# Every second low-part subtraction on GpSimd, and one layer's scale and shift summed on VectorE

## The chip, the cores and the metric

The kernel runs on one core of one Trainium2 chip, as one launch. The metric is the device time of that core in microseconds (us); less is better. The kernel before took 2017.45 us (median of 3 runs, 2016.82 to 2020.26).

## What is computed

The reference is a trunk of two layers over 256 tokens with 2048 features, all in float32. Each layer has a mixer and a feed-forward; each of the four takes `modulate(rmsnorm(x))` and adds its gated output to `x`. Shift, scale and gate come from the conditioning vector `c`: six vectors of 2048 per layer, each `silu(c)` times a 2048x2048 piece of `ada_w`, plus a bias.

```python
cond = jax.nn.silu(c)
for l in range(DEPTH):
    mod = cond @ ada_w[l] + ada_b[l]
    sh1, sc1, g1, sh2, sc2, g2 = jnp.split(mod, N_MOD, axis=-1)
    h = modulate(rmsnorm(x, norm_mix_g[l]), sh1, sc1)
    y = mixer_ab(...) if l % 2 == 0 else mixer_c(...)
    x = x + g1[:, None, :] * y
    h = modulate(rmsnorm(x, norm_ffn_g[l]), sh2, sc2)
    x = x + g2[:, None, :] * swiglu(h, ffn_w1[l], ffn_w3[l], ffn_w2[l])
return rmsnorm(x, final_g)
```

Mixer AB (layer 0) has a projection to 4096 columns, a causal convolution of width 31 over 1024 channels with LayerNorm and SiLU, a gated product with a causal 128x128 mixing of tokens, and a projection back. Mixer C (layer 1) is a causal pooling with one small product per group of channels. The feed-forward is a SwiGLU with 5632 hidden features.

## The kernel before

Tokens stand in two blocks of 128. Every dense product keeps the transposed activations stationary and streams a weight as the moving operand. A product in float32 is made of three in float32r: a weight is cut into `hi = round(w)` and `lo = w - hi`, the activations likewise, and hi*hi, lo*hi and hi*lo are added up in PSUM.

The grain of the work is a unit (`unit`, or `block` for several in one go): SyncE loads 512x512 of a weight (1 MB, `load`, L180) into one of five `raw` buffers; in two halves of 128x1024 `split` (L160) casts `hi` on ScalarE (L165) and subtracts `lo` on VectorE (L166); TensorE then runs, per half, eight matmuls with `hi` (L203, L204) and four with `lo` (L209). There are four `hi` and four `lo` buffers, so the cuts run up to four halves ahead of the products. Up to the end of mixer C the kernel has 184 units: 32 of the projection in, 16 of the projection back, 132 of the first feed-forward and 4 of the pooling mixer. The last feed-forward has another 132.

Two kinds of work run beside the units. `filler` (called five times per half, L167) issues the convolution, which is 31 VectorE instructions for each of 8 channel tiles (L655, L660), and then its LayerNorm. `tick` (L267) issues background steps, 1.2 per unit in mixer AB and 0.71 in the first feed-forward: each step loads 1 MB of `ada_w` for a modulation vector. On TensorE (`on_pe`, L305 and L379) a step is 16 small float32 matmuls, each recorded as two instructions. On VectorE (`weighed`, L349 and L351) it is two passes over 128x1024, `acc = raw * cond + acc`, and TensorE only adds up over the partitions at the end (`put_cols`, L408).

In mixer AB the background order is: the gate g1 on TensorE (L305), then the columns of scale and shift of the first feed-forward on TensorE (`norm_cols` with `mod_cols`, L379), in eight parts of 512 columns. In the first feed-forward it is the gate g2 and the modulation of layer 1, on VectorE. GpSimd has the norms' powers (L472, L748, L690), memsets, and the four bands for mixer C (`bands`, L123 to L149), which are built there during the first feed-forward.

The order of the instructions on each engine comes from a scheduler that takes them by priority as the operands come free; `soon` raises the priority of a phase's entry.

Of the kernel before, what the change touches and what calls it, by code (L numbers as in the profile page):

```python
# [8 lines left out]
F32 = mybir.dt.float32  # L9
# [5 lines left out]
P = 128  # L15
# [23 lines left out]
class Trunk:  # L39
    """Activations stand in [token, feature] blocks of 128 tokens; every dense product keeps  # L40
    the transposed activations stationary and streams a weight as the moving operand.

    A float32 operand w is cut into two float32r parts, hi = round(w) and lo = w - hi, and a
    product is hi*hi + hi*lo + lo*hi, added up in float32 in PSUM."""

    def __init__(self, ctx, tc, ins, out):
        self.ctx, self.tc, self.nc = ctx, tc, tc.nc
        self.i, self.out = ins, out
        self.bg = []
        self.credit = 0.0  # L50
        self.late = []
        self.fill = []

        def pool(name, bufs, **kw):
            return ctx.enter_context(tc.tile_pool(name=name, bufs=bufs, **kw))

        self.cpool = pool("const", 1)
        self.xpool = pool("resid", 1)
        self.apool = pool("act", 1)
        self.rawp = pool("raw", RAW)  # L60
        self.hip = pool("whi", HL)
        self.lop = pool("wlo", HL)
        self.accp = pool("acc", 1)
        self.gp = pool("gate", 2)
        self.wk = pool("work", 2)
        self.mmp = pool("mmp", 4, space=PSUM)
        self.tpp = pool("tpp", 2, space=PSUM)
        self.adap = pool("adap", 1, space=PSUM)
        self.msp = pool("msp", 1, space=PSUM)

# [52 lines left out]
    def bands(self, tiles):  # L123
        """band[w][:, 0 and 1] takes the first 128 tokens to the trailing mean over w tokens
        minus the token, for both halves of the sequence; band[w][:, 2] the second 128 to the
        second half; band[w][:, 3] has the sums over the columns of the first, which from column
        w - 1 on are those of every later token."""
        nc = self.nc
        self.band = {}
        for w, t in zip(WINDOWS, tiles):  # L130
# [3 lines left out]
            # token s (partition) counts for token n (free) when n - w < s <= n  # L134
# [16 lines left out]
    def load_rows(self, src):  # L151
        """A vector as rows of 512 at partitions 0, 32, 64, 96, zeros elsewhere."""
        t = self.wk.tile([P, 512], F32, name="brow", tag="brow", bufs=1)
        self.nc.gpsimd.memset(t, 0.0)
        n = src.shape[0] // 512
        self.nc.sync.dma_start(out=t[0 : 32 * n : 32, :], in_=src.rearrange("(j n) -> j n", n=512))
        return t

# [1 line left out]
    def split(self, raw, h):  # L160
# [5 lines left out]
        nc.vector.tensor_tensor(lo, part, hi.bitcast(F32), op=ALU.subtract)  # L166
# [4 lines left out]
    def filler(self):  # L171
        """One instruction of the work that runs between the cuts of the weights."""
# [15 lines left out]
    def unit(self, w, row0, col0, act, ps, first, last):  # L188
        """ps[b] += act[b] @ w[row0 : row0 + 512, col0 : col0 + 512]; act[b] = (hi, lo)."""
# [23 lines left out]
    def block(self, cells, hooks={}):  # L213
        """Units in one go, the first 128 tokens through all of them before the others.
        hooks[b, n]: what is issued ahead of half unit n of tokens b."""
# [23 lines left out]
    def tail(self, cells, resid, entry):  # L239
        """The last units of a phase: the next one's entry begins with the first 128 tokens  # L240
        while the others are still on."""
# [10 lines left out]
    def soon(self, f, *args):  # L252
        """f(*args), ahead of what else the engines could take up by then."""
        with self.tc.high_priority(SOON):
            f(*args)
# [36 lines left out]
    def mod(self, l, v, on_pe, then):  # L292
        """One modulation vector, silu(c) @ ada_w + ada_b; then(rows) gets it as four rows
        of 512, at partitions 0, 32, 64, 96."""
# [39 lines left out]
    def weighed(self, acc, l, col0):  # L334
        """acc[p, n] = the sum over k of cond[k * 128 + p] * ada_w[k * 128 + p, col0 + n]"""
# [21 lines left out]
    def mod_full(self, l, v, dst, gname=None, halves=(0, 1)):  # L357
        """A modulation vector, or half of it, as columns; see mod_cols."""
# [7 lines left out]
    def mod_cols(self, l, v, q, on_pe, dst, gname=None):  # L366
        """Part q (512 entries) of a modulation vector as columns, dst[p, k] = mod[k * 128 + p],
        or gain * (1 + mod) with a gain."""
# [54 lines left out]
    def to_bcast(self, rows, dst, n=4):  # L423
        """dst[p, :] = vector, on every partition"""
# [11 lines left out]
    def norm_cols(self, e, l, sc, sh, gname, sc_pe, sh_pe):  # L436
        """The columns of gain * (1 + scale) and of shift, in four parts each."""
# [6 lines left out]

    def bcast(self, l, v, on_pe, dst, times=None):
        """A modulation vector (times another) on every partition."""
# [9 lines left out]
    def sumsq(self, b, q):  # L456
        """The squares of a part of the residual, added up as soon as it stands."""
# [17 lines left out]
    def transposed(self, b, q, r):  # L475
        """A PSUM bank with part q of x[b] * r, transposed."""
# [17 lines left out]
    def scaled(self, src, q, b, gs, sh):  # L494
        """gs * src + sh, split: k-tiles 4q to 4q + 3 of the stationary operand."""
# [13 lines left out]
    def prep_norm(self, e, b, q):  # L509
        """act[q][b]: rmsnorm(x) * gain * (1 + scale) + shift, transposed and split."""  # L510
        e.act[q][b] = self.scaled(self.transposed(b, q, e.r[b]), q, b, e.gs, e.sh)

    def prep_late(self, e, b, q):
        """prep_norm, but for the last part, whose scale and shift come later."""
        (self.prep_norm if q < 3 else self.prep_plain)(e, b, q)

    def prep_plain(self, e, b, q):
        """The transposed x * rstd, to wait for scale and shift."""
# [4 lines left out]
    def started(self, e, w_cols, rate, then=None):  # L523
        """The first products of a layer by parts of 512 features, each as soon as its part of
        scale and shift has come."""
# [18 lines left out]
    def begun(self, e, w_cols, rest):  # L544
        """The first products of a layer, over three parts of the features and then over the
        last, as soon as its scale and shift have come."""
# [22 lines left out]
    def to_act(self, src, hi, lo):  # L569
        """src [128 tokens, 512] to split k-tiles."""  # L570
# [17 lines left out]
    def mixer_ab(self, e, nxt):  # L588
        nc, i = self.nc, self.i
        with ExitStack() as s:  # L590
# [19 lines left out]
            def params():  # L610
                """The small parameters of the mixer, laid out."""
# [54 lines left out]
            def norm_a():  # L666
                """LayerNorm over the channels, which stand on the partitions, and SiLU."""
# [45 lines left out]
            # A: gated halves, transposed to [channel, token]  # L713
# [21 lines left out]
            # B: values, normed over channels, mixed over the tokens of a chunk  # L735
# [69 lines left out]
    def prep_pool(self, e, b, g):  # L805
        """The pooling runs along the tokens, so it is a product with a band over them that leaves
        the features on the partitions, where scale and shift then go in: with n = rmsnorm(x),
        band' (gs * n + sh) = gs * (band' n) + sh * (the sums over the band's columns)."""
# [8 lines left out]
        t = self.wk.tile([P, 512], F32, name="xc", tag="xc", bufs=3)  # L817
# [120 lines left out]
    def finish_out(self, b, r):  # L938
        """The last norm; its gain is in already, but for the last part."""
# [12 lines left out]
    def run(self):  # L952
# [24 lines left out]
        self.norm_cols(ffn0, 0, SC2, SH2, "ffn_g", True, True)  # L977
# [4 lines left out]
        with ExitStack() as s:  # L982
# [15 lines left out]
            self.rate = RATES[4]  # L998
            self.g2 = self.gate()
# [6 lines left out]
class Entry:  # L1006
    """What a phase needs before its first product: the norm's factor per 128 tokens, then
    parts of 512 features, prepared one by one."""
# [50 lines left out]
```

## Time and profile before

| | |
|---|---|
| median of 3 runs (lowest, highest) | 2017.45 us (2016.82, 2020.26) |
| profiled execution: span | 2018.1 us |
| TensorE busy | 1961.8 us, 97% |
| VectorE busy | 1384.8 us, 69% |
| ScalarE busy | 837.0 us, 41% |
| GpSimd busy | 36.2 us, 2% |
| mean granted TensorE clock | 0.984 |

The page gives no other time for the profiled execution than its span, which stands 0.65 us above the median. PE is TensorE's matmuls, PEld its weight loads, DVE is VectorE, ACT ScalarE, POOL GpSimd, SP SyncE. Matmuls are pipelined and their ends are modelled, so PE can read as busy while it does not run at its full rate; the number of matmuls in a stretch says more. By lines and times, the program falls into these stages: the start to about 161 us; the convolution beside the first 24 or so units of mixer AB, 161 to 336; the rest of mixer AB, 336 to 443; the first feed-forward, 443 to 1205; mixer C, to about 1260; the last feed-forward, to the end.

### The profile page before, as it was taken

What the parts mean: (1) busy time and instruction counts of PE and PEld (TensorE: products, weight loads), DVE (VectorE), ACT (ScalarE), POOL (GpSimd) and SP (SyncE); (2) the same over time, 40 slices, a digit from 0 to 9 for tenths busy, and PEclk for the clock granted to TensorE, in tenths of its full rate; (3) what the DMA queues carried; (4) which work ended last, traced back from release to release, by engine and by line L of the source; (5) the groups of instructions that cost most, each with busy time, mean ns of one, the idle gap of its engine ahead of it and who ended that gap; (6) DMA issues with size and microseconds to landing.
All of it is one profiled execution on the core that took longest, in us unless ns stands there. A gap on an engine that the chain in (4) does not pass through costs nothing.

```text
span 2018.1 us, 23297 instructions
## 1 busy us (share of the span) xinstructions
PE 1961.8 (97%) x9039; PEld 1542.1 (76%) x9039; DVE 1384.8 (69%) x1660; ACT 837.0 (41%) x1025; POOL 36.2 (2%) x91
## 2 busy tenths in 40 slices
PE   4889999999999999999999999999999999999998
PEld 2457677668887888887878887788788888888886
DVE  3668998556777788777877788777455444554455
ACT  2333333445444343433343346544433444334443
POOL 1000000000000000000120000000000000000000
PEclk7889999999999999999999999999999999999999
DMA  9997887877888898888888886888555555555552
GB/s 327 329 380 278 318 297 285 304 283 254 286 305 316 319 330 321 306 308 313 307 322 303 301 299 232 307 319 312 187 188 187 188 188 188 187 188 190 190 188 78
DMA packets 240159, 540.30 MB, mean 268 GB/s; under 512 B 8393, under 2 KB 9721, under 8 KB 237616
## 3 DMA queue, kind: packets, MB, share of 16 engines
q1 hardware_dynamic: 238264, 536.94, 75.1%
q10 hardware_dynamic: 1784, 1.86, 0.3%
q8 instruction: 71, 1.16, 0.2%
q14 instruction: 40, 0.33, 0.0%
HBM read 536.68 MB, written 2.10 MB: 267 GB/s over the span
## 4 chain that ended last, share of the span: by engine, by line
PE 94%; DVE 2%; DMA 2%; ACT 1%; issue 0%; POOL 0%; POOLq 0%; SPq 0%; ACTq 0%; DVEq 0%
PE mm L203 28%; PE mm L204 28%; PE mm L209 27%; PE ps_ada L379 3%; PE ps_col L408 2%; PE tp L574 1%; DVE accq L388 1%; DMA x<-in_x_dram 1%; PE ps_ada L305 1%; PE mt L204 1%; PE mt L203 1%; PE mt L209 1%; PE tp L823 1%; DVE lo L166 1%; PE tp L482 0%
## 5 line engine op out<-in xcount | busy, mean ns | idle before, releaser
L166 DVE TENSOR_TENSOR lo<-raw,hi 128x1024 fp32r<-128x1024 f32 x632 | 768.4, 1223 | 435.6 <-ACT hi L165 430.7
L165 ACT CAST hi<-raw 128x1024 fp32r<-128x1024 f32 x632 | 661.1, 1053 | 930.9 <-PE mm L204 808.5
L203 PE MATMUL mm<-hi,ah 128*128 128x512 f32 x1600 | 632.3, 395 | 8.6 <-ACT hi L165 7.4
L204 PE MATMUL mm<-hi,al 128*128 128x512 f32 x1600 | 625.9, 391 | 0.0
L209 PE MATMUL mm<-lo,ah 128*128 128x512 f32 x1600 | 431.9, 390 | 2.2 <-DVE lo L166 2.2
L203 PEld LDWEIGHTS mm<-hi,ah 128*128 128x128 f32 x1600 | 301.7, 189 | 96.4 <-ACT hi L165 15.2
L209 PEld LDWEIGHTS mm<-lo,ah 128*128 128x128 f32 x1600 | 301.0, 188 | 66.2 <-DVE lo L166 3.3
L204 PEld LDWEIGHTS mm<-hi,al 128*128 128x128 f32 x1600 | 302.1, 189 | 61.9 <-issue 0.8
L203 PE MATMUL mm<-hi,hh 128*128 128x512 f32 x704 | 279.3, 397 | 0.0
L204 PE MATMUL mm<-hi,hl 128*128 128x512 f32 x704 | 277.9, 395 | 0.0
L351 DVE SCALAR_TENSOR_TENSOR acc<-raw,cond,acc 128x1024 f32<-128x1024 f32 x180 | 230.4, 1280 | 8.7 <-DMA raw<-in_ada_w_dram 7.2
L209 PE MATMUL mm<-lo,hh 128*128 128x512 f32 x704 | 194.6, 395 | 0.0
L203 PEld LDWEIGHTS mm<-hi,hh 128*128 128x128 f32 x704 | 132.1, 188 | 33.4 <-issue 0.8
L209 PEld LDWEIGHTS mm<-lo,hh 128*128 128x128 f32 x704 | 132.1, 188 | 32.2
L204 PEld LDWEIGHTS mm<-hi,hl 128*128 128x128 f32 x704 | 132.1, 188 | 31.2
L660 DVE SCALAR_TENSOR_TENSOR co<-aT,cw,co 128x256 f32<-128x256 f32 x240 | 99.1, 476 | 0.0
L582 DVE TENSOR_TENSOR gy<-mm,gate 128x512 f32<-128x512 f32 x72 | 46.9, 685 | 49.6 <-PE mm L209 49.6
L379 PE MATMUL ps_ada<-raw,cond 128*32 128x512 f32 x448 | 71.8, 677 | 5.6 <-DMA raw<-in_ada_w_dram 5.6
L203 PE MATMUL mm<-hi,mh 128*128 128x512 f32 x160 | 65.9, 413 | 0.0
L204 PE MATMUL mm<-hi,ml 128*128 128x512 f32 x160 | 63.1, 395 | 0.0
L388 DVE SCALAR_TENSOR_TENSOR accq<-raw,cond,accq 128x512 f32<-128x512 f32 x84 | 57.6, 744 | 0.0
L583 DVE TENSOR_TENSOR x<-x,gy 128x512 f32<-128x512 f32 x72 | 47.1, 686 | 0.2
(164 smaller groups left out, 939.9 us busy)
## 6 DMA issues: line engine op xcount, KB each, us to landing
raw<-in_ffn_w_dram SPq DMA_DIRECT2D x264, 1024.0 KB, 5.0
raw<-in_ada_w_dram SPq DMA_DIRECT2D x192, 1024.0 KB, 6.7
raw<-in_ab_w_in_dram SPq DMA_DIRECT2D x32, 1024.0 KB, 6.9
raw<-in_ab_w_out_dram SPq DMA_DIRECT2D x16, 1024.0 KB, 6.1
raw<-in_pool_w_dram SPq DMA_DIRECT2D x4, 1024.0 KB, 5.4
x<-in_x_dram SPq DMA_DIRECT2D x2, 1024.0 KB, 17.6
gate<-in_final_g_dram SPq DMA_DIRECT2D x1, 1024.0 KB
out_dram<-x SPq DMA_DIRECT2D x2, 512.0 KB, 3.7
```

The costliest lines, as they stand in the source:

```text
L165: nc.scalar.copy(hi, part)
L166: nc.vector.tensor_tensor(lo, part, hi.bitcast(F32), op=ALU.subtract)
L203: nc.tensor.matmul(ps[b], act[b][0][:, kk, :], hi[:, k, :], start=first and kk == 0, stop=False)
L204: nc.tensor.matmul(ps[b], act[b][1][:, kk, :], hi[:, k, :], start=False, stop=False)
L209: self.nc.tensor.matmul(ps[b], act[b][0][:, kk, :], lo[:, k, :], start=False, stop=last and kk == 3)
L351: nc.vector.scalar_tensor_tensor(acc, r2[:, j, :], self.cond[:, k : k + 1], acc, op0=ALU.mult, op1=ALU.add)
L379: nc.tensor.matmul(acc[32 * j : 32 * j + 32, :], self.cond[:, k : k + 1].to_broadcast([P, 32]), raw[:, j, :], start=u == 0, stop=u == 3, s ...
L388: nc.vector.scalar_tensor_tensor(acc[:, k % 2, :], raw[:, j, :], self.cond[:, k : k + 1], acc[:, k % 2, :], op0=ALU.mult, op1=ALU.add,)
L408: nc.tensor.matmul(ps[:, a : a + 1], src[:, P * a : P * a + P], one, start=u == 0, stop=u == len(parts) - 1,)
L582: nc.vector.tensor_tensor(t, ps, g[:, 512 * q : 512 * q + 512], op=ALU.mult)
L583: nc.vector.tensor_tensor(xs, xs, t, op=ALU.add)
L660: nc.vector.scalar_tensor_tensor(co[:, k, :], src, cw[:, k, j : j + 1], co[:, k, :], op0=ALU.mult, op1=ALU.add,)
```

## The change

Of the two halves of each unit, the second has its `lo` subtracted on GpSimd instead of VectorE, until the flag `shared` is cleared, which happens after mixer C. The columns of scale and shift of the first feed-forward are no longer summed by TensorE in parts of 512 but by VectorE in halves of 1024 (`norm_halves` with `mod_full`, which the kernel already has for layer 1). The accumulator `acc` gets a second buffer; the tile `xc` of mixer C takes turns in the buffers of `s1` and `hm` instead of three of its own. Comments are left out, which moves line numbers: `lo` is L168 in the changed kernel, the accumulation L351 and L353, the convolution L668 and L673.

```diff
+        self.shared = True
...
-        self.accp = pool("acc", 1)
+        self.accp = pool("acc", 2)
...
         nc.scalar.copy(hi, part)
-        nc.vector.tensor_tensor(lo, part, hi.bitcast(F32), op=ALU.subtract)
+        eng = nc.gpsimd if h and self.shared else nc.vector
+        eng.tensor_tensor(lo, part, hi.bitcast(F32), op=ALU.subtract)
...
+    def norm_halves(self, e, l, sc, sh, gname):
+
+        e.parts = []
+        for hh in range(2):
+            e.parts += [
+                self.add(
+                    self.mod_full(l, sc, e.gs, gname, (hh,)), self.mod_full(l, sh, e.sh, None, (hh,))
+                ),
+                (),
+            ]
...
-        t = self.wk.tile([P, 512], F32, name="xc", tag="xc", bufs=3)
+        t = self.wk.tile([P, 512], F32, name="xc", tag=("s1", "hm")[b])
...
-        self.norm_cols(ffn0, 0, SC2, SH2, "ffn_g", True, True)
+        self.norm_halves(ffn0, 0, SC2, SH2, "ffn_g")
...
             self.mixer_c(mix1, ffn1)
             self.rate = RATES[4]
+            self.shared = False
```

On VectorE, late in the convolution of mixer AB, this is a piece of the order before (`co` is the convolution's output, `lo` the low part of a weight half, `sh` the shift's columns):

```order
L660 SCALAR_TENSOR_TENSOR co<-aT,cw,co 128x256
L166 TENSOR_TENSOR lo<-raw,hi 128x1024
L414 TENSOR_TENSOR sh_140<-ps_col,adab 128x4
L660 SCALAR_TENSOR_TENSOR co<-aT,cw,co 128x256 x7
L166 TENSOR_TENSOR lo<-raw,hi 128x1024
L660 SCALAR_TENSOR_TENSOR co<-aT,cw,co 128x256 x3
L166 TENSOR_TENSOR lo<-raw,hi 128x1024
L660 SCALAR_TENSOR_TENSOR co<-aT,cw,co 128x256 x7
```

The same place on VectorE after the change, just behind the first `bo` pair (`acc` is the new accumulation of the feed-forward's scale and shift):

```order
L673 SCALAR_TENSOR_TENSOR co<-aT,cw,co 128x256 x9
L351 TENSOR_SCALAR acc<-raw,cond 128x1024
L673 SCALAR_TENSOR_TENSOR co<-aT,cw,co 128x256
L353 SCALAR_TENSOR_TENSOR acc<-raw,cond,acc 128x1024
L673 SCALAR_TENSOR_TENSOR co<-aT,cw,co 128x256
L353 SCALAR_TENSOR_TENSOR acc<-raw,cond,acc 128x1024
L168 TENSOR_TENSOR lo<-raw,hi 128x1024
L353 SCALAR_TENSOR_TENSOR acc<-raw,cond,acc 128x1024
L673 SCALAR_TENSOR_TENSOR co<-aT,cw,co 128x256 x8
L353 SCALAR_TENSOR_TENSOR acc<-raw,cond,acc 128x1024
L168 TENSOR_TENSOR lo<-raw,hi 128x1024
```

A subtraction stands there once per unit instead of twice, and about two accumulations per unit have come in. All 64 passes of the accumulation (4 of L351, 60 of L353) stand ahead of the first feed-forward's first subtraction on VectorE.

On GpSimd, from the norm of the start to the entry of the first feed-forward, the order before is this (`r`, `m` and `rv` are the norms' factors, `brow` a buffer for a bias):

```order
L472 TENSOR_TENSOR r<-m,mhalf 128x1 x2
L154 MEMSET brow 128x512
L748 TENSOR_TENSOR m<-m,mhalf 128x1 x2
L690 TENSOR_TENSOR rv<-rv,mhalf 128x2
L472 TENSOR_TENSOR r<-m,mhalf 128x1 x2
```

And after the change, over the same stretch:

```order
L485 TENSOR_TENSOR r<-m,mhalf 128x1 x2
L168 TENSOR_TENSOR lo<-raw,hi 128x1024 x22
L155 MEMSET brow 128x512
L168 TENSOR_TENSOR lo<-raw,hi 128x1024 x3
L761 TENSOR_TENSOR m<-m,mhalf 128x1 x2
L168 TENSOR_TENSOR lo<-raw,hi 128x1024 x10
L703 TENSOR_TENSOR rv<-rv,mhalf 128x2
L168 TENSOR_TENSOR lo<-raw,hi 128x1024 x13
L485 TENSOR_TENSOR r<-m,mhalf 128x1 x2
```

The powers of the norms now stand in one queue with the subtractions, 48 of which lie ahead of the first feed-forward's norm. Over the whole program GpSimd gets 184 of them, one per unit; the bands for mixer C come behind the 145th, in two batches with a single subtraction between them.

## The prediction

> **What bounds the kernel now.** I read the engines' totals first, then the busy time by stage, then the waits, then the single rows where GpSimd and VectorE run at the same time. The totals, from the page:
>
> ```profile
> span 2018.1 us, 23297 instructions
> PE 1961.8 (97%) x9039; PEld 1542.1 (76%) x9039; DVE 1384.8 (69%) x1660; ACT 837.0 (41%) x1025; POOL 36.2 (2%) x91
> ```
>
> TensorE is the bound on average. The windows by stage (convolution; rest of mixer AB; first twelve units of the feed-forward; the rest of it; mixer C; last feed-forward) say where another engine is close. The columns are the stretch and its length, then PE, PEld, DVE, ACT and POOL busy with counts:
>
> ```profile
> 161.00:336.00 175.00, 175.00 (x888) 121.06 (x887) 166.50 (x324) 61.80 (x84) 2.93 (x3) 1.00 0.84 302
> 336.00:443.00 107.00, 107.00 (x543) 76.68 (x542) 60.16 (x76) 42.83 (x62) 1.61 (x1) 0.98 0.84 302
> 443.00:510.00 67.00, 65.24 (x317) 51.82 (x316) 46.22 (x65) 40.64 (x59) 2.00 (x2) 1.00 0.67 233
> 510.00:1205.00 695.00, 695.00 (x3133) 568.09 (x3132) 548.86 (x535) 284.93 (x307) 21.02 (x61) 1.00 0.87 310
> ```
>
> In the convolution stretch VectorE is busy 166.50 of 175 us, 95%: there both engines are full. In the rest of mixer AB it is 60.16 of 107, in the feed-forward 595.08 of 762 (78%). The waits of the whole run, with total, times and longest:
>
> ```profile
> ACT hi L165 <- PE mm L204: 808.5, 491, 6.4
> DVE lo L166 <- ACT hi L165: 430.7, 356, 3.3
> PE mm L203 <- ACT hi L165: 7.4, 3, 4.2
> ```
>
> The cuts wait for TensorE to free their buffers, and TensorE waits only 7.4 us for a cut. So outside the convolution a lighter VectorE gains nothing by itself; what can gain is less work on TensorE.
>
> **What TensorE loses.** L379 in mixer AB is the matmuls of the feed-forward's scale and shift:
>
> ```profile
> 161.00:336.00 175.00, 14.49 (x112) 2.40 (x112) 1.00 0.84 302
> 336.00:443.00 107.00, 15.55 (x120) 2.55 (x120) 0.98 0.84 302
> ```
>
> That is 14.49 + 15.55 = 30.0 us off the path between 161 and 443 us (a few more lie just behind). The column sums stay: 8 parts of 4 small matmuls become 4 of 8. If nothing took its place, the 282 us of mixer AB would become 252, and the run 1988.
>
> **What VectorE gains and loses.** The costs of one instruction (busy us in all, mean ns of one; the last two rows serve further down), and how many cuts lie in each stretch (windows of L166), are
>
> ```profile
> L166 DVE TENSOR_TENSOR lo<-raw,hi 128x1024 fp32r<-128x1024 f32 x632 | 768.4, 1223 | 435.6 <-ACT hi L165 430.7 <-PE mm L209 3.2
> L351 DVE SCALAR_TENSOR_TENSOR acc<-raw,cond,acc 128x1024 f32<-128x1024 f32 x180 | 230.4, 1280 | 8.7 <-DMA raw<-in_ada_w_dram 7.2
> L349 DVE TENSOR_SCALAR acc<-raw,cond 128x1024 f32<-128x1024 f32 x12 | 9.0, 746 | 0.0
> L660 DVE SCALAR_TENSOR_TENSOR co<-aT,cw,co 128x256 f32<-128x256 f32 x240 | 99.1, 476 | 0.0
> L906 DVE TENSOR_TENSOR hm<-s,mm 128x512 f32<-128x512 f32 x44 | 28.3, 682 | 11.9 <-PE mm L209 11.9
> L576 DVE TENSOR_TENSOR hl<-tp,hh 128x512 fp32r<-128x512 f32 x44 | 28.2, 681 | 2.6 <-ACT hh L575 2.6
> ```
>
> ```profile
> 161.00:336.00 175.00, 55.61 (x46) 1.00 0.84 302
> 336.00:443.00 107.00, 33.17 (x28) 0.98 0.84 302
> 443.00:510.00 67.00, 28.10 (x23) 1.00 0.67 233
> 510.00:1205.00 695.00, 293.94 (x241) 1.00 0.87 310
> ```
>
> Mixer AB from 161 us on: half of 74 cuts, 37, leave VectorE: half of 88.78, 44.4 us. In come 60 x 1.280 + 4 x 0.746 = 79.8 us. VectorE's 226.7 us become 262.1. First feed-forward: half of 264 cuts leave, half of 322.0, 161 us; 595.1 become 434.
>
> **What GpSimd costs VectorE.** No row of before shows a 128x1024 subtraction on GpSimd, so its price is bounded, and the first question is whether it runs beside VectorE at all. While the bands are built, VectorE has these rows:
>
> ```profile
> 1003.11 1.28 DVE L582 TENSOR_TENSOR gy<-mm,gate 128x512 f32<-128x512 f32 x2
> 1004.31 1.55 DVE L583 TENSOR_TENSOR x<-x,gy 128x512 f32<-128x512 f32 x2
> 1005.78 1.48 DVE L166 TENSOR_TENSOR lo<-raw,hi 128x1024 fp32r<-128x1024 f32 x1
> ...
> 1008.32 1.30 DVE L351 SCALAR_TENSOR_TENSOR acc<-raw,cond,acc 128x1024 f32<-128x1024 f32 x1
> 1009.55 1.30 DVE L166 TENSOR_TENSOR lo<-raw,hi 128x1024 fp32r<-128x1024 f32 x1
> ```
>
> and GpSimd these:
>
> ```profile
> 1003.81 0.54 POOL L141 TENSOR_SCALAR_AFFINE_SELECT bandhl<-bandhl 128x128 f32<-128x128 f32 x2
> 1004.33 1.85 POOL L145 TENSOR_TENSOR bandhl<-bandhl,ident 128x128 f32<-128x128 f32 x2
> ...
> 1007.25 3.76 POOL L136 TENSOR_SCALAR_AFFINE_SELECT bandhh<-bandhh 128x128 f32<-128x128 f32 x3
> ...
> 1019.23 0.87 POOL L145 TENSOR_TENSOR bandhl<-bandhl,ident 128x128 f32<-128x128 f32 x2
> ```
>
> Beside `gy`, which reads PSUM and one SBUF tile, two selects take 0.54 us. Beside `lo` and `acc`, which read two SBUF tiles, three take 3.76, each about as long as the VectorE instruction it meets. It works both ways: the two `x` additions take 1.55 where the equal pair `gy` takes 1.28, and the `lo` behind them 1.48 where its group's mean is 1.22. Each is 0.26 to 0.27 late, and one subtraction of the bands goes in ahead of each. So I take the two engines as one resource for instructions that read two SBUF tiles: one runs, the other stands. Convolution, cuts, accumulations and the residual's addition are all of that kind.
>
> The price of one new subtraction in this resource: the 128-column one held VectorE for 0.26 to 0.27 us, so 1024 columns hold it for 8 times that, about 2.15 us. The ends come from these rows (min, median and max in ns; and one select over 1024 columns, 1091 ns):
>
> ```profile
> L145 POOL TENSOR_TENSOR bandhl<-bandhl,ident x4: 447/684/978, 1004.3 to 1019.7; 128x128 f32<-128x128 f32 x4
> L612 POOL TENSOR_SCALAR_AFFINE_SELECT prm<-prm 128x1024 f32<-128x1024 f32 x1 | 1.1, 1091 | 11.8 <-DMA prm<-in_b_w_s_dram 11.8
> ```
>
> With one input, 1024 columns took 1.09 us, so about 1.0 is the low end for two; the undisturbed 0.447, times 8, is 3.6, the high end. I take 2.15, since it is the same operation's own hold. The Trainium skill prices it apart from these rows: GPSIMD Engine Reference, section 3.1 (Elementwise), has 4497 ns for an add of 2048 float32 columns, by which I estimate 2.25 us for 1024; no run here shows it, and by it the sum below would be 4 us longer in mixer AB.
>
> **Mixer AB, the sum.** 37 x 2.15 = 79.6 us of GpSimd on top of VectorE's 262.1 is 341.7 us, for a stretch that lasted 282 and in which TensorE now needs 252. What can lie side by side are VectorE's PSUM reads, above all `gy`, with 15 instructions there (windows of L582, the feed-forward's rows for below):
>
> ```profile
> 336.00:443.00 107.00, 9.70 (x15) 0.98 0.84 302
> 443.00:510.00 67.00, 0.69 (x1) 1.00 0.67 233
> 510.00:1205.00 695.00, 14.13 (x22) 1.00 0.87 310
> ```
>
> So 332 to 342; I take 337, which is **55 us longer**. The pair now sets the pace, and the 30 us saved on TensorE vanish under it. What waits then: behind a held VectorE instruction stand `gy` and the next cut, for which TensorE waits; behind a held GpSimd cut the next cut and the norms' powers; and a `raw` buffer stays taken until its last cut is through, so SyncE's next load starts later. Ends: 262.1 + 37 x 1.0 less 9.7 is 289, 7 longer; with 3.6 it is 395, over 100 longer.
>
> **First feed-forward, the sum.** 434 + 132 x 2.15 = 284 makes 718 us, and of GpSimd's 21.0 us there before I count 12 as bands that read SBUF, an estimate: 730 of 762, 96%. Up to 43 of it are PSUM reads that can lie beside GpSimd: 14.8 of `gy`, and of `hm` and `hl` the first feed-forward's half, 14.2 and 14.1. So the pair still fits, but with 4 to 10% to spare, where VectorE had 22%, and with four buffers to even things out. I take **12 us** of stalls, between 0 and 30. One more place is priced apart: the bands stand in GpSimd's queue in two batches, the second about 13 us long (1007.2 to 1020.1 us before), and the next subtraction waits behind it while the cuts are at most four halves ahead, some 11 us at 762 us for 264 halves. **3 us** (0 to 7).
>
> **Entries and mixer C.** The powers of the norms queue behind subtractions on GpSimd, one of them at most still running: up to 2.2 us for each of the entries to the feed-forwards and mixer C, partly covered because the first 128 tokens go ahead while the others are multiplied. The last accumulations stand in between, too. The start is bound by transfers and has eight GpSimd cuts. Together **3 us** (0 to 8). The second `acc` buffer and the tags of `xc` I cost at nothing: the accumulations are in order on VectorE anyway, and `s1` and `hm` are free by then. SyncE's loads stay the same in number and size. Behind mixer C nothing changes.
>
> Sum: 2018.1 + 55 + 12 + 3 + 3 = 2091; the runs' median lies 0.65 under the profile's span, so **2090 us**.
>
> **Rivals.** (A) GpSimd runs beside VectorE, or nearly so, and the change does what its parts promise: faster. Then mixer AB is set by VectorE's 262.1 us, with the 5% of idle time it had in the convolution up to 275, against TensorE's 252: 7 to 20 us less than 282, and with 2 us for GpSimd's longer cut and the entries the run takes about 2006. It decides if the two engines' instructions overlap by more than half: 282 - 262 = 20 us is all that 79.6 us of GpSimd may add. For it speaks only that VectorE is full there; against it speak the stretched rows above. Perfetto Trace Analysis in the Trainium skill, section Optimizing Scalar/DVE Operations, says that with VectorE saturated it may make sense to move work even to GpSimd, and in the next sentence that it might not help between these two, as they share a read port; the trace's rows are on the side of the second sentence.
>
> (B) The hold is over (762 - 446 + 22)/132 = 2.56 us, from which point the pair is over-full in the feed-forward as well, half of the PSUM reads being covered. At 2.7 us mixer AB is 75 longer, the feed-forward 19 plus stalls of 20, and the run takes about 2138. The undisturbed 0.447 x 8 speaks for it, the 0.26 of delay against it.
>
> (C) The hold is near its low end of 1.0 us: mixer AB 7 to 17 longer, the feed-forward free, about 2033. For it speaks that part of the 0.26 may be a fixed cost that does not grow with columns.
>
> **How the numbers follow.** My forecast gets 0.60, A 0.18, B 0.13, C 0.09. About 0.2%, 4 us, is what a measurement of this kernel can tell from no change. A is faster but for 0.02, shared between no change and slower; C has 0.03 in no change. So faster 0.16, same 0.04, slower 0.80. The forecast's own ends (hold of 1.9 to 2.4 us, stalls of 0 to 30) are 2062 to 2126. The range goes from 2012 to 2138: it takes in C and most of B and leaves out A and B's upper part, 2 in 10.
>
> **What would show it.** Right: in the changed profile the subtraction on GpSimd has a mean well over 2 us, and longer still when VectorE's waits are counted in; VectorE's convolution instructions, 0.476 us on average before, get longer, since some wait for GpSimd; mixer AB, from the first convolution to the first feed-forward's norm, lasts 320 to 350 us instead of 282 although TensorE has 30 us less to do; ScalarE's casts wait for VectorE or GpSimd there instead of TensorE. The feed-forward stays within 30 us of 762. Wrong: a GpSimd mean near 1.2 us, unchanged lengths on VectorE, or a mixer AB under 282 us. A feed-forward over 800 us would mean that the pair is over-full there too.

## The result and the profile after

The changed kernel takes **2116.2 us** (median of 4 runs, 2115.9 to 2127.51). The kernel before, run beside it, takes 2018.06 (4 runs, 2016.82 to 2020.26). The ratio is 1.0495, with a 95% interval of 1.0475 to 1.0515: slower by 98 us. The page's head and totals:

```profile
span 2114.3 us, 22894 instructions
PE 1969.5 (93%) x8783; PEld 1566.2 (74%) x8783; DVE 1475.5 (70%) x1534; ACT 831.7 (39%) x1017; POOL 546.5 (26%) x275
```

GpSimd went from 36.2 to 546.5 us. But VectorE, which gave up 184 subtractions, rose from 1384.8 to 1475.5 us. TensorE has 256 matmuls fewer and reads as busy for 8 us longer.

To see where the time went I cut each trace at the same five events: the first and the last convolution instruction, and GpSimd's first norm factor `r` for the first feed-forward, for mixer C and for the last feed-forward. The lengths are in us, worked out from the rows' times:

| stage | before | after | difference |
|---|---|---|---|
| start | 160.5 | 166.6 | +6.1 |
| convolution | 175.9 | 224.5 | +48.6 |
| rest of mixer AB | 106.8 | 117.4 | +10.6 |
| first feed-forward | 768.4 | 795.5 | +27.1 |
| mixer C | 42.4 | 48.0 | +5.6 |
| last feed-forward | 764.0 | 762.4 | -1.6 |

Mixer AB as a whole, the second and third rows, went from 282.7 to 341.9 us. The same stages of the changed kernel as windows (length, then PE, PEld, DVE, ACT and POOL busy, TensorE's granted clock, DMA share, GB/s):

```profile
166.60:391.00 224.40, 185.72 (x804) 134.83 (x803) 221.33 (x328) 61.02 (x81) 91.33 (x28) 0.92 0.67 239
391.00:508.50 117.50, 95.62 (x402) 76.53 (x400) 109.29 (x93) 40.66 (x58) 37.89 (x15) 0.91 0.78 274
508.50:1304.00 795.50, 774.74 (x3449) 631.83 (x3450) 581.56 (x478) 327.24 (x368) 369.45 (x196) 0.98 0.83 294
1304.00:1352.00 48.00, 43.95 (x249) 33.73 (x247) 39.31 (x61) 29.34 (x67) 10.67 (x7) 0.96 0.55 198
1352.00:2114.30 762.30, 751.72 (x3352) 611.49 (x3352) 434.05 (x440) 319.75 (x357) 2.16 (x4) 1.00 0.61 206
```

In the convolution VectorE is recorded busy for 221.33 of 224.40 us and GpSimd for 91.33. That alone does not say whether they worked side by side or whether the records hold waiting; the lengths of the single instructions do. TensorE, full there before, is idle for 39 us. Line by line, from the groups (busy us, mean ns of one):

```profile
L168 DVE TENSOR_TENSOR lo<-raw,hi 128x1024 fp32r<-128x1024 f32 x448 | 589.7, 1320 | 383.7 <-ACT hi L166 377.1 <-PE mm L211 3.2 <-ACT gate L436 2.0
L168 POOL TENSOR_TENSOR lo<-raw,hi 128x1024 fp32r<-128x1024 f32 x184 | 514.3, 2797 | 711.6 <-ACT hi L166 683.4 <-PE mm L211 14.9 <-PE mm L206 13.2
L353 DVE SCALAR_TENSOR_TENSOR acc<-raw,cond,acc 128x1024 f32<-128x1024 f32 x240 | 402.7, 1678 | 85.2 <-DMA raw<-in_ada_w_dram 82.4
L673 DVE SCALAR_TENSOR_TENSOR co<-aT,cw,co 128x256 f32<-128x256 f32 x240 | 127.1, 594 | 0.0
L595 DVE TENSOR_TENSOR gy<-mm,gate 128x512 f32<-128x512 f32 x72 | 47.2, 684 | 22.9 <-PE mm L211 22.8
```

The subtraction that stayed on VectorE went from 1223 to 1320 ns, the accumulation from 1280 to 1678, the convolution from 476 to 594. The gate product `gy`, which reads PSUM and one SBUF tile, has 684, where it had 685. On the single lines (minimum, median and maximum in ns) it shows better than in the means:

```profile
L168 DVE TENSOR_TENSOR lo<-raw,hi x448: 1208/1225/3434, 58.0 to 2093.8; 128x1024 fp32r<-128x1024 f32 x150
L168 POOL TENSOR_TENSOR lo<-raw,hi x184: 2332/2577/9270, 58.2 to 1340.3; 128x1024 fp32r<-128x1024 f32 x184
```

Most subtractions on VectorE take what they took, and some have most of one of GpSimd's in them (3434 is 1208 + 2226). The price of one on GpSimd is its undisturbed length, 2.33 us. TensorE's waits over the whole run (total, times, longest) are

```profile
PE mm L211 <- DVE lo L168: 44.9, 17, 6.7
PE tp L495 <- DVE xr L492: 22.3, 6, 13.3
PE mm L211 <- POOL lo L168: 4.8, 2, 4.0
```

where before they were

```profile
PE tp L482 <- DVE xr L479: 7.4, 4, 5.0
PE mm L209 <- DVE lo L166: 2.2, 2, 1.7
```

It waits for VectorE's cuts much more than for GpSimd's: the longer instruction is mostly not the one that comes late. (Of the 22.3 us for `xr`, the normalized rows, 14.3 lie in the start; of the 4.8 for GpSimd's cuts, 4.0 lie behind the bands.)

### The profile page after: what moved, and what is told of

Its sections match the earlier page's. It is cut to its first block, busy times and chain, and to the rows that moved or that the text cites. A ratio compares the mean times of both kernels' runs of the same rounds, so it can differ in the third digit from the quotient of the medians.

```text
span 2114.3 us, 22894 instructions
## 1 busy us (share of the span) xinstructions
PE 1969.5 (93%) x8783; PEld 1566.2 (74%) x8783; DVE 1475.5 (70%) x1534; ACT 831.7 (39%) x1017; POOL 546.5 (26%) x275
## 5 line engine op out<-in xcount | busy, mean ns | idle before, releaser
L168 DVE TENSOR_TENSOR lo<-raw,hi 128x1024 fp32r<-128x1024 f32 x448 | 589.7, 1320 | 383.7 <-ACT hi L166 377.1
L168 POOL TENSOR_TENSOR lo<-raw,hi 128x1024 fp32r<-128x1024 f32 x184 | 514.3, 2797 | 711.6 <-ACT hi L166 683.4
L211 PE MATMUL mm<-lo,ah 128*128 128x512 f32 x1600 | 440.6, 397 | 37.3 <-DVE lo L168 30.5
L353 DVE SCALAR_TENSOR_TENSOR acc<-raw,cond,acc 128x1024 f32<-128x1024 f32 x240 | 402.7, 1678 | 85.2 <-DMA raw<-in_ada_w_dram 82.4
L205 PEld LDWEIGHTS mm<-hi,ah 128*128 128x128 f32 x1600 | 306.1, 191 | 93.0 <-ACT hi L166 14.7
L485 POOL TENSOR_TENSOR r<-m,mhalf 128x1 f32<-128x1 f32 x10 | 6.9, 694 | 800.1 <-DVE m L483 787.6
L673 DVE SCALAR_TENSOR_TENSOR co<-aT,cw,co 128x256 f32<-128x256 f32 x240 | 127.1, 594 | 0.0
L390 DVE SCALAR_TENSOR_TENSOR accq<-raw,cond,accq 128x512 f32<-128x512 f32 x84 | 71.5, 903 | 5.6 <-DMA raw<-in_ada_w_dram 5.5
L595 DVE TENSOR_TENSOR gy<-mm,gate 128x512 f32<-128x512 f32 x72 | 47.2, 684 | 22.9 <-PE mm L211 22.8
```

Source lines behind the costliest of these rows:

```text
L168: eng.tensor_tensor(lo, part, hi.bitcast(F32), op=ALU.subtract)
L205: nc.tensor.matmul(ps[b], act[b][0][:, kk, :], hi[:, k, :], start=first and kk == 0, stop=False)
L211: self.nc.tensor.matmul(ps[b], act[b][0][:, kk, :], lo[:, k, :], start=False, stop=last and kk == 3)
L353: nc.vector.scalar_tensor_tensor(acc, r2[:, j, :], self.cond[:, k : k + 1], acc, op0=ALU.mult, op1=ALU.add)
L390: nc.vector.scalar_tensor_tensor(acc[:, k % 2, :], raw[:, j, :], self.cond[:, k : k + 1], acc[:, k % 2, :], op0=ALU.mult, op1=ALU.add,)
L595: nc.vector.tensor_tensor(t, ps, g[:, 512 * q : 512 * q + 512], op=ALU.mult)
```

## The experiments

Three theories. **Port**: the forecast's, that an instruction of VectorE with two SBUF inputs and one of GpSimd that reads SBUF take turns, so their times add up. **Latency**: the engines run side by side, and a half's `lo` merely comes later, because GpSimd takes longer over it. **Load**: GpSimd is innocent, and the 80 us of sums laid on a full VectorE are what costs. The first three runs take the change apart, the next three change the GpSimd instruction itself, and the last four test single terms. Unless said otherwise a kernel stands 2 to 4 runs against the 12 to 23 of before that were made beside it.

**Sharing alone** (the sums stay on TensorE):

```diff
-        self.norm_halves(ffn0, 0, SC2, SH2, "ffn_g")
+        self.norm_cols(ffn0, 0, SC2, SH2, "ffn_g", True, True)
```

> The changed kernel with the feed-forward's scale and shift back on TensorE; the GpSimd subtractions stay. Three theories. Port: VectorE and GpSimd instructions that read two SBUF tiles exclude each other, so their times add up: in mixer AB 227 - 44 + 37 x 2.35 = 270 us of the pair, some 10 of it PSUM reads, against 282 of TensorE: it just fits, 0 to 10 us longer; the first feed-forward 27 longer as in the changed kernel, start and mixer C 10 together: 2055 to 2065 us. Latency: GpSimd's cut is slow by itself and TensorE waits for it, whatever VectorE has to do: all of the loss stays and the 30 us of TensorE come back, 2110 to 2145. Load: the accumulations alone overfill VectorE, and GpSimd costs nothing: 2013 to 2023.

2090.7 us, ratio 1.0348 (1.0326 to 1.0371). A miss by some 26 us. The first feed-forward is 796.0 us as with both parts; mixer AB is 311.8, although its pair of engines has less to do than 282 us: 226.7 - 44.4 + 39 x 2.33 = 273. The order on VectorE says why: before, the last of the 248 convolution instructions stands behind 68 cuts, two per unit, so 34 units are cut by then; in the changed kernel behind 34, one per unit, so 34 units again; here behind 29, so only 29 units. (In all three 11 of these units are cut before the convolution begins.) Five units of TensorE's work are moved behind the convolution. The two parts of mixer AB, cut at the end of the convolution:

```profile
168.00:338.00 170.00, 150.37 (x711) 102.42 (x710) 168.86 (x288) 50.11 (x70) 74.94 (x23) 0.96 0.69 248
338.00:480.00 142.00, 141.80 (x725) 100.76 (x724) 67.57 (x75) 55.25 (x77) 49.32 (x21) 0.99 0.85 303
```

The first is full on VectorE and has 711 matmuls instead of before's 888; the second is full on TensorE (141.80 of 142), with VectorE at 67.57. What was held up in the first could not be made good in the second, where TensorE is the bound. A sum over the whole of mixer AB does not see that.

**The sums alone** (the change with no sharing):

```diff
-        self.shared = True
+        self.shared = False
```

> The changed kernel with all subtractions on VectorE; scale and shift are summed on VectorE. Port: no GpSimd in it, so mixer AB is VectorE's 227 + 80 = 306 us, at the 95% it reached before up to 322, against 282: 2043 to 2058 us; the first feed-forward as before. Latency: nothing slow is left and TensorE has 30 us less: 1988 to 1998. Load: the whole loss is here, 2100 or more.

2052.44 us, ratio 1.0184 (1.0152 to 1.0216), as expected. Mixer AB is 315.6 us against VectorE's 226.7 + 79.8 = 306.5 worked out in the forecast; the feed-forward, 769.4, is 1 us from before's 768.4. So of the two parts each is a loss by itself.

**Sharing in the first feed-forward and mixer C alone** (sums on TensorE):

```diff
         self.mixer_ab(mix0, ffn0)
...
+        self.shared = True
```

> GpSimd subtractions only in the first feed-forward and mixer C; scale and shift on TensorE as before. Port: the first feed-forward loses the 27 us it lost in the changed kernel, mixer C 6; mixer AB as before: 2045 to 2055 us. Latency: 136 of the 184 cuts are slow, about three quarters of a loss of 98 to 128: 2090 to 2110. Load: 2013 to 2023.

2050.27 us, ratio 1.0159 (1.014 to 1.0178), as expected. Mixer AB is 282.7 us to the tenth, the feed-forward 793.2 (+24.8), mixer C 47.9 (+5.5). The stalls in the feed-forward come from sharing, and have nothing to do with mixer AB.

**Two memsets in place of each subtraction** (`lo` of those halves is zero, so the lo*hi product of half the weights is left out):

```diff
-        eng = nc.gpsimd if h and self.shared else nc.vector
-        eng.tensor_tensor(lo, part, hi.bitcast(F32), op=ALU.subtract)
+        if h and self.shared:
+            for _ in range(2):
+                nc.gpsimd.memset(lo.bitcast(F32), 0.0)
+        else:
+            nc.vector.tensor_tensor(lo, part, hi.bitcast(F32), op=ALU.subtract)
```

> The changed kernel, but GpSimd does not subtract: it clears the low part twice (two memsets of 128x1024, 0.96 us each before), so it is busy about 1.9 us per unit and reads no SBUF; the low part of every second half is left out of the products. Port: writing alone does not hold the port, so VectorE's 262 us rule mixer AB, 262 to 275 instead of 282, and the feed-forward is as before: 2000 to 2012 us. Latency: GpSimd is busy nearly as long per cut, so most of the loss stays: 2080 or more. Load: the accumulations overfill VectorE still: 2100.

2023.74 us (10 runs), ratio 1.0022 (1.001 to 1.0034). GpSimd is nearly as long busy per half, 1.93 us, but it only writes. The groups:

```profile
L169 POOL MEMSET lo<- 128x1024 f32 x368 | 355.5, 967 | 779.2 <-PE mm L214 755.3 <-PE mt L214 13.5
L171 DVE TENSOR_TENSOR lo<-raw,hi 128x1024 fp32r<-128x1024 f32 x448 | 547.0, 1223 | 477.3 <-ACT hi L166 472.9 <-PE mm L214 3.0
L356 DVE SCALAR_TENSOR_TENSOR acc<-raw,cond,acc 128x1024 f32<-128x1024 f32 x240 | 307.5, 1281 | 79.6 <-DMA raw<-in_ada_w_dram 76.4
L676 DVE SCALAR_TENSOR_TENSOR co<-aT,cw,co 128x256 f32<-128x256 f32 x240 | 98.4, 475 | 0.0
```

VectorE's three lengths are those of before within a nanosecond, beside 355.5 us of GpSimd, and mixer AB falls from 341.9 to 278.8 us. Load is out as the whole cause: the sums are all still on VectorE. (The sums do cost some 33 us when all the cuts stay on VectorE as well, as their run alone showed.) The Trainium skill, SBUF — State Buffer, section Who interferes with whom, has it that a VectorE instruction with two SBUF inputs is in the way of a GpSimd one that reads SBUF, not of one that only writes. The trace agrees, 475 ns beside the memsets against 594 beside the subtractions. A memset waits for no cast, so this `lo` is also ready earlier than a subtracted one: against the latency theory it is VectorE's lengths that speak here, and the doubled subtraction below, not the time.

The time itself missed the port theory's 2000 to 2012 by 12 us. Most of that, 9.1 us, is the first feed-forward (777.5 us), which was to stay as before: 5 of it are lost at the bands, where TensorE waits 3.1 us once for a low part that stands behind them in GpSimd's queue. That loss needs no port. Mixer AB is 4 us above the 275 at which its range ended; that is taken up under the half of the sums.

**One input in place of two** (a cast of the raw half on GpSimd; `lo` then holds the weight itself, so the product is another one):

```diff
-        eng.tensor_tensor(lo, part, hi.bitcast(F32), op=ALU.subtract)
+        nc.gpsimd.tensor_copy(lo, part)
```

> The changed kernel, but GpSimd copies the weight half into the low part instead of subtracting: one input instead of two, about 1.1 us as its select over 1024 columns; the products are those of a wrong low part. Port: the hold falls to 1.0 us, mixer AB 262 + 38 less 10 is 290 to 300, 8 to 18 us longer, the feed-forward's pair 434 + 132 + 12 = 578 of 768 is free again: 2030 to 2048 us. Latency: the cut is as fast as VectorE's own, and TensorE's 30 us are saved: 1988 to 2005. Load: 2100.

2042.38 us (2 runs), ratio 1.0113 (1.0091 to 1.0134), as expected. Mixer AB is 292.7 us. The cast takes 1.03 us undisturbed (minimum, median and maximum in ns):

```profile
L168 POOL CAST lo<-raw x184: 1031/1044/6989, 56.5 to 1268.1; 128x1024 fp32r<-128x1024 f32 x184
```

**Every GpSimd subtraction twice** (the second repeats the first; the product is unchanged):

```diff
         eng.tensor_tensor(lo, part, hi.bitcast(F32), op=ALU.subtract)
+        if h and self.shared:
+            eng.tensor_tensor(lo, part, hi.bitcast(F32), op=ALU.subtract)
```

> The changed kernel with every GpSimd subtraction done twice. Port: 4.7 us of hold per unit: mixer AB 262 + 37 x 4.7 less 10 = 426, 145 longer than before; the feed-forward 434 + 12 + 132 x 4.7 = 1066, less up to 43: 255 to 298 longer; start and mixer C 25: 2440 to 2490 us. Latency: a delay twice as long per cut, at most twice the loss of 98: 2200 to 2220. Load: 2116, no change, since GpSimd has the time.

2449.68 us (one run, so without an interval), in the port theory's range and 230 us above latency's. By stage:

```profile
180.40:462.40 282.00, 197.91 (x799) 143.02 (x798) 276.96 (x328) 61.17 (x81) 149.64 (x54) 0.84 0.56 195
462.40:610.50 148.10, 104.71 (x407) 83.49 (x405) 134.75 (x93) 40.78 (x58) 76.37 (x27) 0.83 0.61 214
610.50:1626.20 1015.70, 845.36 (x3445) 667.72 (x3444) 898.68 (x478) 326.03 (x368) 822.77 (x328) 0.91 0.66 231
```

Mixer AB is 430.1 us. With the change and the cast that makes three points on one line. GpSimd has 38 of the cuts in this stretch (25 and 13 by the windows of the subtraction, in the change as here; 37 with the cast), and d is the undisturbed length of what it does per cut: 1.03, 2.33 and 4.66 us. With 253.3 chosen to fit, 253.3 + 38 x d gives 292.4, 341.8 and 430.4; measured 292.7, 341.9 and 430.1. The slope is one: every microsecond that GpSimd works there is added to the stage. The first feed-forward says the same: 434 + 12 + 132 x 4.66 = 1061 us for the pair, less up to 43 of PSUM reads, is 1018; it took 1015.7, where GpSimd's 615 us alone would have fitted into 768. Two engines side by side do not do that, nor do cuts that only come late. Latency is out.

**Half of the sums on VectorE, no sharing**, and **a quarter of them**: taken from the kernel before, to see whether less of the sums would have gained anything by itself.

```diff
-        self.norm_cols(ffn0, 0, SC2, SH2, "ffn_g", True, True)
+        self.norm_mixed(ffn0, 0, SC2, SH2, "ffn_g")
...
+    def norm_mixed(self, e, l, sc, sh, gname):
+        e.parts = [
+            self.add(self.mod_cols(l, sc, q, True, e.gs, gname), self.mod_cols(l, sh, q, True, e.sh))
+            for q in range(2)
+        ]
+        e.parts.append(
+            self.add(self.mod_full(l, sc, e.gs, gname, (1,)), self.mod_full(l, sh, e.sh, None, (1,)))
+        )
+        e.parts.append(())
```

> The kernel before with only the second half (1024 columns) of the feed-forward's scale and shift summed on VectorE, the first half on TensorE, no GpSimd subtractions. These accumulations fall into the rest of mixer AB, where VectorE had 60 of 107 us. Port: VectorE 60 + 40 = 100, TensorE 107 - 15 = 92: 100 to 107, the run 2010 to 2018 us. Latency: only TensorE's gain counts, 2003. Load: slower than before, 2025 or more.

2018.83 us (12 runs), ratio 0.9996 (0.9986 to 1.0006): no change, just above the port theory's 2010 to 2018. With a quarter, `mod_cols(..., q < 3, ...)` for all four parts:

> The kernel before with only the last 512 columns of scale and shift summed on VectorE (32 passes over 128x512, 0.74 us each, 24 us), three quarters on TensorE, no GpSimd subtractions. Port: VectorE 60 + 24 = 84 in the rest of mixer AB, TensorE 107 - 7.5 = 99.5 rules: 2009 to 2013 us. Latency: the same. Load: 2018 or more.

2023.37 us (11 runs), ratio 1.0017 (1.0008 to 1.0025): a miss by about 10 us, and no gain either. Mixer AB took 284.1 and 282.5 us, against 282.7 before, though TensorE had 15 and 7.5 us less to do. Its rest, after the convolution, in the kernel with half of the sums, and then its casts' and TensorE's waits there:

```profile
333.60:441.90 108.30, 99.56 (x441) 78.95 (x439) 94.81 (x103) 42.95 (x61) 1.70 (x2) 0.94 0.85 307
```

```profile
ACT hi L165 <- DMA raw<-in_ab_w_out_dram: 22.9, 7, 7.0
...
PE mm L209 <- DVE lo L166: 6.8, 4, 2.8
```

TensorE has some 100 matmuls fewer than before's 543, and the stretch is no shorter: VectorE is at 94.81 of 108.3, TensorE waits for its cuts, and the casts wait 22.9 us for loads of the projection's weight (before 16.4), with the same traffic as before (0.85 of the DMA engines, 307 GB/s; before 0.84 and 302). So the rows read as if mixer AB had three bounds close to each other, TensorE, VectorE and the loads, so that what is taken off one is not gained. No run isolated that: with a quarter of the sums VectorE is busy for only 76.04 of the 106.6 us behind the convolution, and why nothing was gained there stays open. With the memsets VectorE has 262 us to do and the stage takes 278.8. In the convolution VectorE is full (175.33 of 179.0 us), behind it not (83.88 of 99.9), so the difference lies mostly behind it.

**Sharing in the last part of mixer AB alone** (from the projection back on, sums on TensorE, no sharing elsewhere):

```diff
+            self.shared = True
             out_half(1)
...
             out_half(0)
+            self.shared = False
```

> Scale and shift on TensorE; GpSimd subtractions only in the 16 units of the projection back, behind the convolution. It asks where the run with sharing everywhere and no accumulations lost its 29 us of mixer AB: its loss showed behind the convolution (141.5 instead of 106.8 us). Port, with the work displaced: that stretch was long only because the convolution had been put ahead and kept the port, so that five units more were left; sharing in it costs nothing, since 60 - 19 + 16 x 2.35 = 79 us of the pair stand against 107: 2016 to 2024 us. Latency: the cuts are slow where they are shared, 2040 to 2053.

2023.91 us (9 runs), ratio 1.0026 (1.0016 to 1.0035); mixer AB 288.8 us. The time is within the port theory's 2016 to 2024. Behind the convolution VectorE has slack, and sharing there costs 6 us of the stage, where the theory had nothing; by subtraction that leaves to the convolution 23 of the 29 us that sharing alone added to mixer AB.

**Sharing in the feed-forward, but not around the bands** (as the third kernel, with VectorE subtracting both halves from the unit in which GpSimd begins on the bands until after they are built):

```diff
+                if gi == 1 and l == 0 and n == 3:
+                    self.shared = False
...
+                if gi == 2 and l == 0 and ci == 0:
+                    self.shared = True
```

> Sharing in the first feed-forward and mixer C only, as in the run of that kind (2050 us), but not in the 12 units around the bands, so that no cut waits in GpSimd's queue behind them. Port and queue: the two stalls of TensorE at the bands, 7.7 and 3.8 us in that run's trace, go, the rest of the loss stays: 2036 to 2042 us. If the loss is spread evenly over the shared cuts: 12 of 132 fewer, 2047 to 2049.

2033.27 us, ratio 1.0061 (1.0038 to 1.0084), 17 us less than the third kernel by medians, and 3 below the range that was forecast. The feed-forward is 779.6 us, 13.6 less. With the subtractions in the queue, the stretch around the bands in the third kernel, what GpSimd does there (start, length) and TensorE's longest wait are

```profile
1014.00:1070.00 56.00, 45.31 (x179) 34.47 (x178) 31.38 (x28) 18.39 (x21) 38.09 (x67) 0.88 0.70 249
```

```profile
1018.56 3.43 POOL L168 TENSOR_TENSOR lo<-raw,hi 128x1024 fp32r<-128x1024 f32 x1
...
1024.05 2.59 POOL L142 TENSOR_SCALAR_AFFINE_SELECT bandhh<-bandhh 128x128 f32<-128x128 f32 x2
...
1034.97 0.86 POOL L146 TENSOR_TENSOR bandhl<-bandhl,ident 128x128 f32<-128x128 f32 x2
1035.80 6.97 POOL L168 TENSOR_TENSOR lo<-raw,hi 128x1024 fp32r<-128x1024 f32 x3
```

```profile
PE mm L211 <- POOL lo L168: 7.3, 1, 7.3
```

Between 1021.94 and 1035.80 us GpSimd has nothing but bands; three cuts stand behind them and take 7 us more in one go. In the changed kernel itself it looks the same: TensorE is busy for 35.02 of the 44 us from 1089 to 1133, waits 4.0 us there for GpSimd's cut and 4.9 for a broadcast's operand, and its granted clock is 0.88. Left out of the queue, the same stretch has no hole:

```profile
990.00:1060.00 70.00, 68.58 (x298) 54.71 (x297) 55.45 (x51) 28.48 (x31) 31.22 (x62) 1.00 0.88 314
```

## Why the prediction was right, and which sizes were off

The forecast of 2090 with 2012 to 2138 had the sign, the mechanism and the order of size; the result is 26 us above it. By its steps, with the terms measured in the traces:

- **Mixer AB, +55 forecast, +59.2 measured.** Shown: the pair is one resource (the memsets leave VectorE alone, and the three points lie on a slope of one). A subtraction holds it for 2.33 us where I had taken 2.15. The estimate of 2.25 us worked out from the Trainium skill (GPSIMD Engine Reference, section 3.1) was the nearer. The pair then has 262.1 + 38 x 2.33 = 351 us of work, and the stage took 341.9: 9 less, about the 9.7 of `gy` that the forecast had put beside GpSimd. The line's 253.3 at d = 0 is that 262 less 9.
- **One step of it was luck.** I added up the pair over the whole of mixer AB. For the change that holds, because the pair is over-full in both parts of it. In sharing alone it isn't, and the same sum missed by 26 us: VectorE's convolution fills its queue until 338 us, and TensorE pays afterwards.
- **The 30 us off TensorE "vanish under it".** Right, and more so than I wrote: half of the sums gained nothing with no GpSimd near. Neither TensorE's 252 us nor the 262 to 275 that rival A counted on came with a free port; with it free (the memsets) the stage took 278.8.
- **First feed-forward, +12 of stalls and +3 for the bands forecast, +27.1 measured.** Sharing in this phase without the bands costs 779.6 - 768.4 = 11.2 us, so the stalls had the right size. But that was luck: they were forecast for a pair that is 96% full, cut after cut, and they are not there. Followed from cast to cast of `hi`, the changed kernel loses 7.1 us in the first 12 casts of the feed-forward, 0.3 in the next 188 (537.1 against 536.8 us), 13.2 in the ten at the bands and the other 6 in the last 54, towards mixer C. The four buffers evened the pair out; besides the bands the loss sits at the two ends. The kernel without the bands loses in lumps too, 5 of its 11 us at one place. What makes up these lumps was not taken apart. **The bands are the term that was mis-sized**: 13.6 us (in the third kernel, 793.2 - 779.6) instead of 3, outside its 0 to 7. I set a batch of 13 us against 11 us of cover from four buffers. But the first batch has used up part of the cover already: the single cut between the two landed at 1021.94, and TensorE was through with what it had at 1030.86, 8.9 us later. The second batch then takes 13.9 (some of its selects stand against VectorE, as they did before: 2.59 us for two that take 0.54 unhindered), and the cut behind it another 2.3 before TensorE has its `lo` at 1038.18. That is a hole of 7.3 us, and a smaller one of 3.4 follows at a broadcast. The memsets lose 5 us at this place with no port in it, so part of the term is the queue alone.
- **Entries, mixer C and start, +3 forecast, +11.7 measured.** Mixer C's 5.6 come from sharing (47.9 to 48.0 in all kernels that share there with subtractions, 42.4 in those that don't, 42.6 with the cast, 43.2 with the memsets, 55.4 with two subtractions). The start is open: it took 157.0 to 165.2 us even in kernels that share nothing there, 166.6 and 168.1 with the subtractions shared there, and 180.4 with two of them.
- **The base.** The changed kernel's profiled execution took 2116.14 us with a span of 2114.3, so a run stands 1.8 us above its span. I had set the run 0.65 below it, comparing two different executions. That is 2.5 us of the 26; the terms above, with the last feed-forward's -1.6, make up the other 23 (96 between the two traces' spans against 73).
- **What would show it.** The mean of GpSimd's cut is over 2 us (2.80), `co` got longer (476 to 594 ns), mixer AB lies within 320 to 350. The feed-forward's 795.5 us are 27.1 above the 768.4 that it had by the cut used here, but 33.5 above the 762 that I had named. The sign of the casts did not come: I had them wait for VectorE or GpSimd instead of TensorE. In mixer AB they wait mostly for loads, as they did before (35.0 and 16.4 us, with 21.3 for `co`), only longer. The waits over mixer AB after the change:

```profile
ACT hi L166 <- DMA raw<-in_ab_w_in_dram: 61.0, 9, 9.6
...
ACT hi L166 <- DMA raw<-in_ab_w_out_dram: 39.1, 8, 10.2
PE mm L211 <- DVE lo L168: 39.0, 16, 6.7
...
ACT hi L166 <- DVE co L673: 27.5, 4, 10.8
```

The DMA engines are less busy there than before (0.67 and 0.78 against 0.84), so the longer waits fit loads that start later because their `raw` buffers come free later; no run isolates that.

Of the rivals, A (side by side) fell with the lengths: stretched beside the subtractions, unchanged beside the memsets. B (a hold of over 2.56 us) fell with the undisturbed 2.33, though the time lies 22 us from B's 2138 and 26 from 2090: the lengths decide that, not the total. C (near 1.0) fell with the same number; 1.03 is what one input takes.

## What to carry to other kernels

Moving element-wise work with SBUF inputs from VectorE to GpSimd is no relief to VectorE where its own work has two SBUF inputs: add the two up as one engine, with GpSimd's undisturbed length (here 2.33 against 1.22 us), before looking at whose total is smaller. Make that sum by stage and in the order in which the queue stands, not over a phase. And what is put into the queue of an engine that has a rare long job, as GpSimd has the bands, must be covered for that job and its own backlog together.

## What the runs showed of the hardware that was not expected

**Turns are not taken instruction by instruction.** I had expected the waiting engine to get its turn when the other's instruction ends. In the changed kernel, GpSimd and then VectorE in the convolution:

```profile
195.91 11.80 POOL L168 TENSOR_TENSOR lo<-raw,hi 128x1024 fp32r<-128x1024 f32 x2 [6.63 <-ACT hi L166]
```

```profile
193.40 8.39 DVE L673 SCALAR_TENSOR_TENSOR co<-aT,cw,co 128x256 f32<-128x256 f32 x21
201.71 1.21 DVE L168 TENSOR_TENSOR lo<-raw,hi 128x1024 fp32r<-128x1024 f32 x1
202.85 2.61 DVE L673 SCALAR_TENSOR_TENSOR co<-aT,cw,co 128x256 f32<-128x256 f32 x1
```

The first of the two subtractions, from 195.91 us, took 9.27 us (the maximum above): VectorE ran 14 convolution instructions and a subtraction through at their undisturbed pace, 8.39 us for 21, and the next one then took 2.61 in its turn. It goes the other way as well; beside GpSimd's last two band rows and the three cuts behind them (6.99 us for three, its undisturbed 2.33) VectorE stood with one accumulation for 8.93 us:

```profile
1092.64 0.86 POOL L146 TENSOR_TENSOR bandhl<-bandhl,ident 128x128 f32<-128x128 f32 x2
1093.47 6.99 POOL L168 TENSOR_TENSOR lo<-raw,hi 128x1024 fp32r<-128x1024 f32 x3
```

```profile
1092.60 10.25 DVE L353 SCALAR_TENSOR_TENSOR acc<-raw,cond,acc 128x1024 f32<-128x1024 f32 x2 [5.39 <-DMA raw<-in_ada_w_dram]
```

So an engine with a stream of instructions and no wait between them can keep the other out for several of them. What ends the turn is not shown. In the second place GpSimd's stream was over; in the first VectorE's rows have no gap ahead of the instruction that took 2.61 us. In all seven places of this trace where a GpSimd subtraction took over 4 us, the VectorE instruction that stood at its end is the one right behind a `lo` of VectorE. The sum over a stage stays the same, but a single cut can be 7 us late.

**TensorE's clock fell with the stalls.** The granted clock in the two windows of mixer AB is 0.92 and 0.91 (before 1.00 and 0.98), and 0.84 and 0.83 with two subtractions; the waits there reach 6.7 us. The Trainium skill (TensorE: Matmul & The Clock Gate, Part 1) has TensorE at half rate after an idle window of about 3.4 us. The trace is in keeping with that, as its waits reach 6.7 us and its means lie between half and full. No run isolates what it cost; since the three points lie on a line of slope one with clocks from 0.96 (the cast) down to 0.83, it is argued, not shown, that it is little in that stage, where TensorE isn't the bound.
